# Down product of a SwiGLU layer: sums added into the residual by accumulating transfers, from copies made by ScalarE

## The chip, the cores and the metric

The kernel runs on one core of one Trainium2 chip. A core has a matrix engine (TensorE, PE in the profile; its weight loads are PEld), a vector engine (VectorE, DVE), a scalar engine (ScalarE, ACT), a general engine (GpSimd, POOL) and a synchronisation engine (SyncE, SP). Here SP only issues transfers (DMAs); the transfers themselves run on 16 DMA engines. Matrix products are written to PSUM, a small memory of 8 banks of 128 x 512 float32; everything else lies in SBUF. The metric is device time in microseconds (us) of one execution, lower is better.

## What is computed

A decoder layer: an input projection, two kinds of attention, an output projection and a feed-forward block, on 256 tokens of width 2048. The change lies in the feed-forward block (D_FF = 5632):

```
h = x + jnp.concatenate([gla_out, nsa_out], axis=-1) @ w_out
m = rms_norm(h, ffn_norm_g)
return h + (jax.nn.silu(m @ w_gate) * (m @ w_up)) @ w_down
```

All inputs and the output are float32.

## The kernel before

**Precision.** A float32 product is made from three matmuls of a faster 32-bit format: each operand is split into an upper part (copied into the format) and a lower part (what the copy lost), and upper x upper, upper x lower and lower x upper are summed in PSUM. `in_parts` (L563 to L565) does the split: ScalarE copies the upper part (L564), VectorE subtracts to get the lower part (L565).

**Tiling.** The residual `h_sb` is four tiles of [128, 2, 512] (two token tiles, 512 columns each). The hidden width 5632 is cut into 11 blocks of 512, numbered f = 0 to 10. The main loop (L1076 to L1082) runs gate_up(f) and then down(f-1); after gate_up(10) come down(9) and down(10).

**gate_up** (L949) walks over 8 pairs of 128-row weight tiles, in the order 0, 1, 2, 4, 3, 5, 6, 7 from f = 1 on (`ORDER`). Pairs 0, 2, 4, 5 and 6 are done with seven products in place of eight (a 2 x 2 scheme of Strassen's kind, 21 matmuls): for them VectorE also makes sums of weights (L983, L984, L985), and the split covers the weights (three quarters of the tile, here called w) and the sums (here called s, two splits). The other pairs take 24 matmuls and one split of the whole tile. At the end of the last seven-product pair the seven sums are combined from the PSUM banks (L1007 to L1012); at the end of the block the rest follows (L1019 to L1025). Those tiles come from the pool tag `f2` with 10 buffers of 512 columns.

**down** (L1041) multiplies one block of 512 hidden units by four column blocks n = 0 to 3 of `w_down`, 24 matmuls each, into two PSUM banks each (one per token tile). When a column block is done, VectorE adds each bank to the residual in place (L1055). In the last call the additions are made in halves of 256 columns, and each half is sent to the output (L1057).

**Weights** come in through `load4` (L928) into the tag `fraw`, 3 buffers of 1 MB, in two transfers of 512 KB (gate and up) or one of 1 MB (down); `two_parts` gives the 4 buffers of the tag `ftwo` for the split parts. A `fraw` buffer is free for the next load when VectorE and ScalarE have read it, an `ftwo` buffer when the matmuls that read it are done.

**Order.** When the kernel is built, the framework's scheduler puts the instructions of each engine in one fixed order, and the engine works them off in that order. An instruction that waits for another engine or for a transfer holds back what stands behind it. SP's transfers are issued in the order of the loads.

Of the kernel before, what the change touches and what calls it, by code (L numbers as in the profile page):

```python
# [11 lines left out]
AF = mybir.ActivationFunctionType  # L12
ALU = mybir.AluOpType
AX = mybir.AxisListType

P = 128
S = 256
NT = S // P
# [18 lines left out]
def kernel(  # L37
# [4 lines left out]
    nc = tc.nc  # L42
    act, mm = nc.scalar.activation, nc.tensor.matmul
    TT, TS, STT = nc.vector.tensor_tensor, nc.vector.tensor_scalar, nc.vector.scalar_tensor_tensor
# [12 lines left out]
    def slot(pool, tag, bufs, align=None):  # L57
        def f(shape, dt=F32):
            n_tiles[0] += 1
            return pool.tile([P] + list(shape), dt, tag=tag, bufs=bufs, name=f"{tag}_{n_tiles[0]}", align_bytes=align)  # L60
        return f
# [3 lines left out]
    g4, g2, g1, small = slot(gp, "g4", 24, LINE), slot(s2p, "g2", 13), slot(s1p, "g1", 7), slot(s1p, "sm", 12)  # L65

    def bank():
        n_tiles[0] += 1
        return pp.tile([P, 512], F32, tag="bank", name=f"bank_{n_tiles[0]}")
# [36 lines left out]
    last = {}  # L106
# [85 lines left out]
    def transpose(o, i, n=P):  # L192
        return nc.tensor.transpose(o, i, ident[:n, :n])  # L193
# [369 lines left out]
    def in_parts(hi, lo, ps):  # L563
        act(hi, ps, AF.Copy)  # L564
        TT(lo, ps, f32(hi), ALU.subtract)  # L565
# [273 lines left out]
    h_sb = []  # L839
# [32 lines left out]

    def pair_forms(pair, v):

        f = g2([4, P])
        a0, a1, b0, b1 = v[:, 0, :P], v[:, 0, P:], v[:, 1, :P], v[:, 1, P:]
        TT(f[:, 0], b1, a1, ALU.subtract)
        TT(f[:, 1], f[:, 0], b0, ALU.subtract)
        TT(f[:, 2], b0, b1, ALU.subtract)
        TT(f[:, 3], a0, f[:, 1], ALU.add)  # L880
        r = forms[pair] = g4([2, 4, P], F32R)
        in_parts(r[:, 0], r[:, 1], f)
# [32 lines left out]
    rf = kp.tile([P, NT], F32, name="rf")  # L915
    fw = {}

    def ffn_pools():
        nonlocal g2, small
        for pool in (wp, s2p, s1p, cp):  # L920
            pool.release()
        fr = ctx.enter_context(tc.tile_pool(name="fr", bufs=1, reuse_waits="tile"))
        fs = ctx.enter_context(tc.tile_pool(name="fs", bufs=1, reuse_waits="tile"))
        fp = ctx.enter_context(tc.tile_pool(name="fp", bufs=1, reuse_waits="tile"))
        fw["raw"], fw["two"] = slot(fr, "fraw", 3, LINE), slot(fp, "ftwo", 4, LINE)
        g2, small = slot(fs, "f2", 10), slot(fs, "fm", 4)

    def load4(parts):  # L928

        r, at = fw["raw"]([4, 512]) if fw else weight("raw", 4, 512, 3, F32), 0  # L930
        for mat, k0, nk, c0 in parts:
            nc.sync.dma_start(r[:, at:at + nk], mat[k0 * P:(k0 + nk) * P, c0:c0 + 512].rearrange("(k p) w -> p k w", p=P))
            at += nk
        return r

    def two_parts():
        w = fw["two"]([2, 4, 512], F32R)
        return w[:, 0], w[:, 1]
# [10 lines left out]
    def gate_up(fb, aTs, before):  # L949

        hi, lo = g4([4, S], F32R), g4([4, S], F32R)
        aTs.append((hi, lo))
        banks = {}

        def product(q, a, w, k):

            if q not in banks:
                banks[q] = bank()
                new = True
            else:  # L960
                new = False
            for i, (x, m) in enumerate(((a[0], w[k][0]), (a[0], w[k][1]), (a[1], w[k][0]))):
                todo[q] -= 1
                mm(banks[q], x, m, start=new and i == 0, stop=todo[q] == 0)  # L964

        def tokens(k, t):
            assert k in turned
            return tuple(x[k // 4][:, k % 4, t * P:(t + 1) * P] for x in (hT_h, hT_l))

        order, sevens = (ORDER0, FIRST7) if fb == 0 else (ORDER, PAIRS7)  # L970
        last7 = max(sevens, key=order.index)
        todo = dict.fromkeys((1, 5, 6, 7), 3 * len(sevens))
        todo.update(dict.fromkeys((2, 3, 4), 3 * len(sevens) + 6 * (8 - len(sevens))))
        todo[8] = 6 * (8 - len(sevens))
        for at, pair in enumerate(order):
            if fb == 0 and at == len(OLD):
                ffn_pools()
            a, b = 2 * pair, 2 * pair + 1
            r = load4([(m[0], a, 2, fb * FB) for m in (w_gate, w_up)])
            if pair in sevens:  # L980
                w = parts_of(r[:, 0:3])
                s1, s2 = g4([2, 512]), g4([2, 512])
                TT(s1, r[:, 1:3], r[:, 3:4].to_broadcast([P, 2, 512]), ALU.add)  # L983
                TT(s2[:, 0], s1[:, 1], r[:, 1], ALU.add)  # L984
                TT(s2[:, 1], s2[:, 0], r[:, 0], ALU.add)  # L985
                f = [tuple(forms[pair][:, i, j] for i in range(2)) for j in range(4)]
                product(1, tokens(b, 0), w, 1)
                yield 2
                product(2, tokens(a, 0), w, 0)
                yield 2  # L990
                product(3, f[3], w, 2)
                yield 2
                hi_, lo_ = two_parts()
                in_parts(hi_[:, 0:2], lo_[:, 0:2], s1)
                in_parts(hi_[:, 2:4], lo_[:, 2:4], s2)
                w = [(hi_[:, k], lo_[:, k]) for k in range(4)]
                for q, x, k in ((5, f[0], 0), (7, f[2], 1), (6, f[1], 2), (4, tokens(a, 1), 3)):
                    product(q, x, w, k)
                    yield 2
            else:  # L1000
                w = parts_of(r)
                for q, t, m in ((2, 0, 0), (3, 0, 1), (4, 1, 0), (8, 1, 1)):
                    for j in range(2):
                        product(q, tokens(a + j, t), w, 2 * m + j)
                        yield 2
            if pair == last7:
                q1, u, q5u, q7u, q57u = (g2([512]) for _ in range(5))  # L1007
                act(q1, banks[1], AF.Copy)
                TT(u, banks[6], q1, ALU.add)
                TT(q5u, banks[5], u, ALU.subtract)  # L1010
                TT(q7u, banks[7], u, ALU.add)
                TT(q57u, banks[5], q7u, ALU.subtract)  # L1012
                if before is not None:
                    urgent.append(before)
        if fb == 0:
            drain(urgent)
            rms(rf, ssh)
            TT(rf, rf, hback, ALU.mult)
        gs = []  # L1019
        for t, (g, gq, u_, uq) in enumerate(((q1, 2, q5u, 3), (q7u, 4, q57u, 8))):  # L1020
            TT(g, banks[gq], g, ALU.add)
            act(g, g, AF.Silu, scale=rf[:, t:t + 1])
            TT(u_, banks[uq], u_, ALU.add)
            STT(g, u_, rf[:, t:t + 1], g, ALU.mult, ALU.mult)
            gs.append(g)  # L1025
        turns[fb] = turn_act(gs, hi, lo)

    turns = {}

    def turn_act(gs, hi, lo):  # L1030
        for t in range(NT):
            ts = slice(t * P, (t + 1) * P)
            p = bank()
            for j in range(4):
                transpose(p[:, j * P:(j + 1) * P], gs[t][:, j * P:(j + 1) * P])
                if j % 2:
                    yield
            pv = p.rearrange("p (j s) -> p j s", j=4)
            in_parts(hi[:, :, ts], lo[:, :, ts], pv)

    def down(f0, aTs, last):  # L1041

        for m in range(2):
            banks = [[bank() for _ in range(NT)] for _ in range(2)]
            for f, (ah, al) in enumerate(aTs):
                end = f == len(aTs) - 1
                for i, n in enumerate((2 * m, 2 * m + 1)):
                    ws = parts_of(load4([(w_down[0], 4 * (f0 + f), 4, n * 512)]))
                    yield from chunk([banks[i]], ah, al, ws, f == 0, end, t_first=last and end)
                    if not end:  # L1050
                        continue
                    for t in range(NT):
                        for c in range(0, 512, 256 if last else 512):
                            cs = slice(c, c + (256 if last else 512))
                            TT(h_sb[n][:, t, cs], banks[i][t][:, cs], h_sb[n][:, t, cs], ALU.add)  # L1055
                            if last:
                                nc.sync.dma_start(out[t * P:(t + 1) * P, n * 512 + c:n * 512 + c + 256], h_sb[n][:, t, cs])  # L1057


    drive([proj(C_LR, ev_go(0), ((0, 256), (256, 272)), first_chunk)], 2)  # L1060
# [50 lines left out]
```

## Time and profile before

| | |
|---|---|
| median of 3 runs | 1134.25 us (1134.21 to 1136.03) |
| the profiled execution, its own time | 1134.1 us |
| its span, first to last instruction | 1132.4 us |
| granted clock of TensorE, mean | 0.999 of full |
| TensorE busy | 1120.4 us (99%) |
| VectorE busy | 965.9 us (85%) |
| ScalarE busy | 619.8 us (55%) |
| GpSimd busy | 23.6 us (2%) |
| bytes moved by transfers | 213.45 MB, 189 GB/s over the span |

From 516.78 us on, the profile repeats: one round is down(f-1) followed by gate_up(f+1), and nine such rounds follow each other until 1082.72 us, with down(9) and down(10) behind them. In the timelines below a row has start, duration, engine, line, operation, output and input with their shapes, and the number of instructions merged into the row; in brackets stands the idle time before it and what ended it.

### The profile page before, as it was taken

Reading aid. Unit: us, or ns where it says so; the run is one execution under the profiler, and the core shown is the slowest. Engines: PE = TensorE matmul, PEld = TensorE weight load, DVE = VectorE, ACT = ScalarE, POOL = GpSimd, SP = SyncE. Lnnn points to the kernel's source line nnn. Section 1 sums busy time; section 2 is a strip of 40 time slices with the busy share of each in tenths; the row PEclk is TensorE's granted clock in tenths of the full one; section 3 lists DMA queues with packets and bytes.
Section 4 is the critical chain, followed back from the end, with each engine's and each line's share of the span. In section 5 each row is a group of like instructions: output and inputs, shape, how many; then the busy total and the mean of one; then the engine's idle time right before and its main releaser. Section 6 shows DMA issues by size and latency. Waiting matters only on the chain.

```text
span 1132.4 us, 14359 instructions
## 1 busy us (share of the span) xinstructions
PE 1120.4 (99%) x5515; PEld 927.1 (82%) x5515; DVE 965.9 (85%) x1205; ACT 619.8 (55%) x763; POOL 23.6 (2%) x53
## 2 busy tenths in 40 slices
PE   9999999999999999999999999999999999999998
PEld 8888889998777777788888888888888888888886
DVE  6547779987588678999999999999999999999993
ACT  7654466544466486664555546364555555464640
POOL 3000000100000000000000000000000000000000
PEclk9999999999999999999999999999999999999999
DMA  7655543445853354556665656555565556565652
GB/s 269 233 186 186 186 149 114 152 151 152 299 182 112 112 186 149 184 193 219 221 224 180 225 180 233 186 202 193 199 208 200 207 166 223 185 243 168 196 211 75
DMA packets 110446, 213.45 MB, mean 189 GB/s; under 512 B 5109, under 2 KB 8217, under 8 KB 110378
## 3 DMA queue, kind: packets, MB, share of 16 engines
q1 hardware_dynamic: 110378, 212.54, 56.1%
q8 instruction: 43, 0.70, 0.2%
q14 instruction: 25, 0.20, 0.1%
HBM read 210.42 MB, written 2.10 MB: 188 GB/s over the span
## 4 chain that ended last, share of the span: by engine, by line
PE 89%; issue 4%; DVE 4%; DMA 1%; POOL 0%; SPq 0%; ACT 0%; POOLq 0%; DVEq 0%
PE bank L261 45%; PE bank L964 37%; PE bank L193 3%; PE bank L817 1%; PE bank L759 1%; DVE ftwo L565 1%; DMA raw<-in_w_out_dram 1%; DVE lo L130 1%; DMA g<-in_x_dram 1%; PE bank L513 1%; DVE g L515 0%; DVE g L518 0%; DVE g L490 0%; PE bank L675 0%; DVE g L489 0%
## 5 line engine op out<-in xcount | busy, mean ns | idle before, releaser
L964 PE MATMUL bank<-ftwo,g 128*128 128x512 f32 x1905 | 444.9, 392 | 1.3 <-DVE ftwo L565 1.1
L964 PEld LDWEIGHTS bank<-ftwo,g 128*128 128x128 f32 x1905 | 354.0, 188 | 75.4 <-DVE ftwo L565 2.2
L261 PE MATMUL bank<-hi,g 128*128 128x512 f32 (+3 forms) x1152 | 326.3, 366 | 0.8 <-DVE g L615 0.6
L564 ACT ACTIVATE ftwo<-fraw 128x1536 fp32r<-128x1536 f32 (+1 forms) x130 | 226.3, 1741 | 141.5 <-PE bank L261 41.2
L565 DVE TENSOR_TENSOR ftwo<-fraw,ftwo 128x1536 fp32r<-128x1536 f32 (+1 forms) x130 | 267.2, 2067 | 13.8 <-ACT ftwo L564 13.8
L261 PE MATMUL bank<-ftwo,g 128*128 128x512 f32 x1056 | 241.9, 389 | 0.0
L261 PEld LDWEIGHTS bank<-ftwo,g 128*128 128x128 f32 x1056 | 198.0, 188 | 41.6 <-DVE g L565 0.4
L261 PEld LDWEIGHTS bank<-hi,g 128*128 128x128 f32 x1152 | 199.3, 189 | 30.9 <-issue 2.3
L130 DVE TENSOR_TENSOR lo<-raw,hi 128x1024 fp32r<-128x1024 f32 (+3 forms) x125 | 151.4, 1218 | 74.5 <-ACT hi L129 74.0
L564 ACT ACTIVATE ftwo<-g 128x1024 fp32r<-128x1024 f32 x106 | 110.5, 1058 | 158.9 <-DVE g L983 75.2
L261 PE MATMUL bank<-lo,g 128*128 128x512 f32 (+1 forms) x576 | 195.3, 365 | 0.5 <-DVE lo L130 0.5
L129 ACT ACTIVATE hi<-raw 128x1024 fp32r<-128x1024 f32 (+3 forms) x125 | 131.3, 1056 | 109.3 <-PE bank L261 77.5
L565 DVE TENSOR_TENSOR ftwo<-g,ftwo 128x1024 fp32r<-128x1024 f32 x106 | 127.2, 1217 | 8.2 <-ACT ftwo L564 8.2
L261 PEld LDWEIGHTS bank<-lo,g 128*128 128x128 f32 x576 | 102.6, 189 | 15.0 <-issue 0.9
L1055 DVE TENSOR_TENSOR g<-bank,g 128x512 f32<-128x512 f32 (+1 forms) x96 | 59.3, 642 | 15.6 <-PE bank L261 14.7
L983 DVE TENSOR_TENSOR g<-fraw 128x1024 f32<-128x1024 f32 x53 | 64.5, 1216 | 0.0
L564 ACT ACTIVATE g<-bank 128x512 fp32r<-128x512 f32 (+1 forms) x50 | 29.2, 587 | 21.8 <-PE bank L193 12.5
L193 PE MATMUL bank<-ident,g 128*128 128x128 f32 (+2 forms) x214 | 38.4, 278 | 2.4 <-DVE g L548 1.1
L565 DVE TENSOR_TENSOR g<-bank,g 128x512 fp32r<-128x512 f32 (+1 forms) x50 | 33.6, 681 | 7.7 <-ACT g L564 7.4
L193 PEld LDWEIGHTS bank<-ident,g 128*128 128x128 f32 (+2 forms) x214 | 27.5, 142 | 12.3 <-issue 2.3
L985 DVE TENSOR_TENSOR g<-g,fraw 128x512 f32<-128x512 f32 x53 | 36.3, 685 | 0.6
L984 DVE TENSOR_TENSOR g<-g,fraw 128x512 f32<-128x512 f32 x53 | 36.3, 685 | 0.5
(192 smaller groups left out, 639.3 us busy)
## 6 DMA issues: line engine op xcount, KB each, us to landing
fraw<-in_w_down_dram SPq DMA_DIRECT2D x44, 1024.0 KB, 5.1
fraw<-in_w_gate_dram SPq DMA_DIRECT2D x86, 512.0 KB, 3.8
fraw<-in_w_up_dram SPq DMA_DIRECT2D x86, 512.0 KB, 4.7
raw<-in_w_in_dram SPq DMA_DIRECT2D x36, 1024.0 KB, 5.1
raw<-in_w_out_dram SPq DMA_DIRECT2D x16, 1024.0 KB, 5.1
raw<-in_w_in_dram SPq DMA_DIRECT2D x4, 1072.0 KB
g<-in_x_dram SPq DMA_DIRECT2D x7, 512.0 KB, 9.8
raw<-in_w_in_dram SPq DMA_DIRECT2D x3, 1056.0 KB, 11.4
```

What stands on the lines that cost most here:

```text
L129: act(h[:, i:i + n], r[:, k + i:k + i + n], AF.Copy)
L130: TT(o[:, i:i + n], r[:, k + i:k + i + n], f32(h[:, i:i + n]), ALU.subtract)
L193: return nc.tensor.transpose(o, i, ident[:n, :n])
L261: last["mm"] = mm(bk[t], a[:, k, t * P:(t + 1) * P], m[:, off:off + w], start=(first_ and k == 0 and i == 0), stop=(end and k == 3 and i = ...
L513: mm(p[:, j * P:(j + 1) * P], u, w, start=True, stop=True)
L564: act(hi, ps, AF.Copy)
L565: TT(lo, ps, f32(hi), ALU.subtract)
L964: mm(banks[q], x, m, start=new and i == 0, stop=todo[q] == 0)
L983: TT(s1, r[:, 1:3], r[:, 3:4].to_broadcast([P, 2, 512]), ALU.add)
L984: TT(s2[:, 0], s1[:, 1], r[:, 1], ALU.add)
L985: TT(s2[:, 1], s2[:, 0], r[:, 0], ALU.add)
L1055: TT(h_sb[n][:, t, cs], banks[i][t][:, cs], h_sb[n][:, t, cs], ALU.add)
```

## The change

The 80 additions of L1055 in all calls of `down` but the last are replaced. ScalarE copies the two banks of a column block into an SBUF tile `step` [128, 2, 512] (two buffers), and GpSimd issues a transfer of 512 KB from `step` to `h_sb[n]` that adds to what is there. To make room in the pool, the ten 2 KB buffers `f2` become two of 4 KB for `gate`, one of 4 KB for `up` and two of 4 KB for `step`; gate_up's combining steps are the same operations, written into halves of `gate` and `up`. The last call of `down` keeps its additions and its output transfers.

```
-        f = g2([4, P])
+        f = fw["up"]([4, P]) if fw else g2([4, P])
...
-        g2, small = slot(fs, "f2", 10), slot(fs, "fm", 4)
+        fw["up"], fw["step"] = slot(fs, "up", 1), slot(fs, "step", 2)
+        g2, small = slot(fs, "gate", 2), slot(fs, "fm", 4)
...
-                q1, u, q5u, q7u, q57u = (g2([512]) for _ in range(5))
-                act(q1, banks[1], AF.Copy)
-                TT(u, banks[6], q1, ALU.add)
-                TT(q5u, banks[5], u, ALU.subtract)
-                TT(q7u, banks[7], u, ALU.add)
-                TT(q57u, banks[5], q7u, ALU.subtract)
+                gate, up = g2([NT, 512]), fw["up"]([NT, 512])
+                act(gate[:, 0], banks[1], AF.Copy)
+                TT(up[:, 1], banks[6], gate[:, 0], ALU.add)
+                TT(up[:, 0], banks[5], up[:, 1], ALU.subtract)
+                TT(gate[:, 1], banks[7], up[:, 1], ALU.add)
+                TT(up[:, 1], banks[5], gate[:, 1], ALU.subtract)
...
+                    if not last:
+                        step = fw["step"]([NT, 512])
+                        for t in range(NT):
+                            act(step[:, t], banks[i][t], AF.Copy)
+                        nc.gpsimd.dma_start(h_sb[n], step, accum_op=ALU.add)
+                        continue
                     for t in range(NT):
-                        for c in range(0, 512, 256 if last else 512):
-                            cs = slice(c, c + (256 if last else 512))
+                        for c in range(0, 512, 256):
+                            cs = slice(c, c + 256)
                             TT(h_sb[n][:, t, cs], banks[i][t][:, cs], h_sb[n][:, t, cs], ALU.add)
-                            if last:
-                                nc.sync.dma_start(out[t * P:(t + 1) * P, n * 512 + c:n * 512 + c + 256], h_sb[n][:, t, cs])
+                            nc.sync.dma_start(out[t * P:(t + 1) * P, n * 512 + c:n * 512 + c + 256], h_sb[n][:, t, cs])
```

As built, the changed program has 80 instructions more on ScalarE, 80 fewer on VectorE and 40 transfers on GpSimd's queue, behind all its other work. TensorE's matmuls and SP's loads stand in the same order. On VectorE and ScalarE the fixed order around the pairs of gate_up moved as well. VectorE's order in a round, from pair 1 to pair 3 (lower parts written as "lo", the weight sums by line, old line numbers):

```
before: lo p0 s, lo p1, L1055 x2, L984 p2, lo p2 w, L985 p2, lo p2 s, L983 p4, lo p2 s, lo p4 w,
        L984 p4, L983 p5, L985 p4, L984 p5, lo p4 s x2, L985 p5, lo p3
after:  lo p0 s x2, L983 to L985 p2, L983 p4, L984 p4, lo p1, L985 p4, lo p2 w, lo p2 s x2, lo p4 w,
        L983 to L985 p5, lo p4 s x2, L983 p6, lo p3
```

ScalarE's copies for column blocks 0 to 3 stand ahead of its splits of pair 0 w, pair 0 s, pair 1 and pair 2 w.

More of the change, by code (lines that the diff above doesn't have):

```diff
@@ L1018, in gate_up, with turn_act @@
             TT(rf, rf, hback, ALU.mult)
-        gs = []
-        for t, (g, gq, u_, uq) in enumerate(((q1, 2, q5u, 3), (q7u, 4, q57u, 8))):
+        for t, (gq, uq) in enumerate(((2, 3), (4, 8))):
+            g, u = gate[:, t], up[:, t]
             TT(g, banks[gq], g, ALU.add)
             act(g, g, AF.Silu, scale=rf[:, t:t + 1])
[L1023 to L1026, printed above, removed]
+            TT(u, banks[uq], u, ALU.add)
+            STT(g, u, rf[:, t:t + 1], g, ALU.mult, ALU.mult)
+        turns[fb] = turn_act(gate, hi, lo)
     turns = {}
-    def turn_act(gs, hi, lo):
+    def turn_act(gate, hi, lo):
         for t in range(NT):
@@ L1034, in turn_act @@
             for j in range(4):
-                transpose(p[:, j * P:(j + 1) * P], gs[t][:, j * P:(j + 1) * P])
+                transpose(p[:, j * P:(j + 1) * P], gate[:, t, j * P:(j + 1) * P])
                 if j % 2:
```

## The prediction

> **What bounds the kernel now.** First the page's busy times, then the windows, cut at the rounds, then the chain of waits inside one round.
>
> ```profile
> PE 1120.4 (99%) x5515; PEld 927.1 (82%) x5515; DVE 965.9 (85%) x1205; ACT 619.8 (55%) x763; POOL 23.6 (2%) x53
> ```
>
> ```profile
> core 0: us, PE busy (x) PEld busy (x) DVE busy (x) ACT busy (x) POOL busy (x), PEclk, DMA share, GB/s
> 705.33:768.19 62.86, 62.86 (x282) 51.93 (x282) 59.98 (x58) 33.73 (x27) 0.00 (x0) 1.00 0.60 201
> ...
> 831.04:894.17 63.13, 63.13 (x282) 51.85 (x282) 60.57 (x59) 33.94 (x28) 0.00 (x0) 1.00 0.59 199
> ...
> 1082.72:1132.40 49.68, 44.60 (x201) 36.40 (x199) 28.54 (x37) 11.29 (x8) 0.00 (x0) 0.97 0.31 110
> ```
>
> ```profile
> 705.33 21.76 PE bank L261 x96
> 727.09 36.04 PE bank L964 x159
> 764.26 1.39 PE bank L964 x6
> 766.80 1.39 PE bank L964 x6
> 768.19 21.76 PE bank L261 x96
> ...
> 1087.38 39.95 PE bank L261 x176
> ```
>
> In a round TensorE never pauses: 96 matmuls in 21.76 us and 159 in 36.04 are 226.7 ns each, and the next round's first matmul starts as the last one ends. VectorE, from which the change takes work, is at 59.98 of 62.86 us, close to a bound without being one. Where it is less loaded (the last window, 28.54 of 49.68) the matmuls are no quicker: 176 in 39.95 us, 227.0 ns each. So less work on VectorE has nothing to shorten. What can be won is the little that is lost: 63.13 - 62.86 = 0.27 us in one round.
>
> The Trainium skill (Trainium Kernel Development and Optimization, Performance Expectations) warns that busy time of matmuls is a bad metric of distance to the roofline, since they are pipelined. By that rule 99% busy could hide waiting that VectorE causes. The trace does not agree: 226.7 ns in both halves of a round, and no less behind the rounds.
>
> **What is removed and added.** By form:
>
> ```profile
> L1055 DVE TENSOR_TENSOR g<-bank,g 128x512 f32<-128x512 f32 x80 | 53.3, 686 | 3.3 <-PE bank L261 2.4
> L1008 ACT ACTIVATE f<-bank 128x512 f32<-128x512 f32 x11 | 6.4, 584 | 1.2 <-PE bank L964 1.2
> ```
>
> Removed: 80 additions of 686 ns, 53.3 us of VectorE, 5.3 us a round. Worth nothing by itself, as said. Added: 80 copies from PSUM to SBUF of the kind of L1008, 80 x 0.584 = 46.7 us of ScalarE, 4.7 a round, which brings it to 38.4 of 62.86. Its time is no bound; its place may be. Write T for the start of a round's first matmul (705.33). A column block takes 24 x 0.2267 = 5.44 us, so the copies can run at T + 5.44, 10.88, 16.32 and 21.76, and ScalarE stands still for them. Behind them wait its splits:
>
> ```profile
> 710.86 1.49 ACT L564 ACTIVATE ftwo<-fraw 128x1536 fp32r<-128x1536 f32 x1 [2.91 <-issue]
> 718.19 1.06 ACT L564 ACTIVATE ftwo<-g 128x1024 fp32r<-128x1024 f32 x1 [5.84 <-DVE g L983]
> ...
> 721.74 1.92 ACT L564 ACTIVATE ftwo<-fraw 128x2048 fp32r<-128x2048 f32 x1 [1.11 <-PE bank L261]
> 727.46 1.49 ACT L564 ACTIVATE ftwo<-fraw 128x1536 fp32r<-128x1536 f32 x1 [3.80 <-PE bank L261]
> ```
>
> These are pair 0's w and first s, pair 1 and pair 2's w; all but the s already began right when the same column blocks ended (T + 5.5, 16.4, 22.1), because they need the buffer that those matmuls free. Each now comes some 1 us later: pair 2 at T + 21.85 + 2 x 0.55 = 23.0. TensorE wants pair 2 at T + 21.76 + 45 x 0.2267 = 31.96. Free. The PSUM banks that the copies release are wanted no sooner: the last pair of them, free at T + 23.0, by the seventh product of gate_up at T + 21.76 + 18 x 0.2267 = 25.84.
>
> Also added: 40 transfers of 512 KB from SBUF to SBUF that add. The trace has no transfer from GpSimd and none that adds. Two numbers matter: how long one takes to land (L), and how much time of the 16 DMA engines it eats (a). A round loads 12 MB (8 pairs and 4 column blocks) at a share of 0.60 of 62.86 us: 37.7 us, 3.1 us a MB. As a plain copy, a = 1.6 us is the low end; since the destination must be read too, twice the reading gives a = 3.1, and this I take, as nearer to what such a transfer does. For L:
>
> ```profile
> fraw<-in_w_gate_dram SPq DMA_DIRECT2D x86, 512.0 KB, 3.8
> fraw<-in_w_up_dram SPq DMA_DIRECT2D x86, 512.0 KB, 4.7
> ...
> g<-in_x_dram SPq DMA_DIRECT2D x7, 512.0 KB, 9.8
> ```
>
> 3.8 us is the low end, 9.8 (512 KB in a crowd of loads) the high end; I take about 3.8 + 1.6 = 5.4, for the second reading.
>
> The Trainium skill (Collectives: The Full Stack, The bandwidth ceiling: the fold count and why AG ≠ RS ≠ AR) says that an adding step runs at half the rate of a copy, because two sources are read. That speaks against this change; by it a is 3.1 too. No run before shows it.
>
> `step` has two buffers: the copy of block 2 at T + 16.4 needs block 0's transfer, issued at about T + 6.7, landed. Free up to L = 9.6; and up to about 12.9 TensorE would not feel it (block 3's first copy, 0.58, behind block 1's transfer of T + 12.3, for the bank wanted at T + 25.84). At 5.4, nothing. On GpSimd's queue nothing stands behind a transfer but the next one, 5.44 us later.
>
> **Where the stall goes.** What I hold to decide is VectorE's order around pairs 4, 5 and 3. Before:
>
> ```profile
> 724.05 2.28 DVE L565 TENSOR_TENSOR ftwo<-fraw,ftwo 128x2048 fp32r<-128x2048 f32 x1
> 726.45 1.37 DVE L1055 TENSOR_TENSOR g<-bank,g 128x512 f32<-128x512 f32 x2
> ...
> 728.98 1.76 DVE L565 TENSOR_TENSOR ftwo<-fraw,ftwo 128x1536 fp32r<-128x1536 f32 x1 [0.56 <-ACT ftwo L564]
> 730.65 0.69 DVE L985 TENSOR_TENSOR g<-g,fraw 128x512 f32<-128x512 f32 x1
> ...
> 736.93 1.22 DVE L983 TENSOR_TENSOR g<-fraw 128x1024 f32<-128x1024 f32 x1
> ...
> 739.27 2.35 DVE L565 TENSOR_TENSOR ftwo<-g,ftwo 128x1024 fp32r<-128x1024 f32 x2
> 741.54 0.68 DVE L985 TENSOR_TENSOR g<-g,fraw 128x512 f32<-128x512 f32 x1
> 742.15 3.95 DVE L565 TENSOR_TENSOR ftwo<-fraw,ftwo 128x2048 fp32r<-128x2048 f32 x2
> ```
>
> ```profile
> 726.36 0.37 SPq L932 DMA_DIRECT2D fraw<-in_w_gate_dram  x1
> ...
> 731.41 0.37 SPq L932 DMA_DIRECT2D fraw<-in_w_gate_dram  x1
> 731.82 0.47 SPq L932 DMA_DIRECT2D fraw<-in_w_up_dram  x1
> ```
>
> The row at 724.05 is pair 1's lower part, 728.98 pair 2's, 736.93 pair 5's first sum, 742.15 pair 3's lower part (2.28 of the 3.95), done at T + 39.1. Pair 3's second matmul needs it at T + 21.76 + 88 x 0.2267 = 41.7: a margin of 2.6 us, the smallest that I find in gate_up. SP loads pair 3 when pair 1's lower part is done (726.36) and pair 5 when pair 2 is through (731.41, T + 26.1), so pair 5's up half lands at about 731.82 + 4.7 = T + 31.2, just before its use at T + 31.6.
>
> After, with the durations of these rows: pair 2's split on ScalarE is 0.9 later, done at T + 24.5; its lower part, with L985 now done ahead, ends at T + 24.5 + 1.76 = 26.3, and pair 5's load goes out as before. VectorE is through with pair 2's s and pair 4's w at T + 26.3 + 2.35 + 1.76 = 30.4 and now stands at pair 5's three sums, with pair 4's s, pair 6's first sum and pair 3 behind them. If pair 5 lands at T + 31.3 + d, pair 3's lower part is there 1.22 + 2 x 0.69 + 2.35 + 1.22 + 2.28 = 8.45 later, at T + 39.7 + d. So TensorE stalls by d - 2.0 in each round.
>
> And d is there. Block 3's transfer goes out at about T + 23.2. Pair 3's load is later than before, next to it, since pair 1's lower part now stands behind L983 and L984 of pair 4: VectorE gets to these at about T + 12.1 (block 1's copies) + 1.06 + 2.35 (pair 0's s) + 2.6 (pair 2's sums) = 18.1, and they need pair 4's load, which goes out when pair 0 is through (T + 6.7 + 1.49 + 1.76 + 2.6 = 12.5) and lands 0.41 + 4.7 = 5.1 later at best, beside block 1's transfer. So pair 1 is done, and pair 3 loads, at T + 18.1 + 1.22 + 0.69 + 2.28 = 22.3, or 23.5 with crowding, where it was T + 21.0. Pair 3 takes 3.1 us of engine time and pair 5 follows 2.7 to 3.9 us behind, so block 3's a is passed on to pair 5 less some 0.5: d = 1.1 for a = 1.6, 2.6 for a = 3.1. The stall is 0 at the low end and 0.6 us at the value taken.
>
> **Sum.** Nine rounds have a gate_up behind a changed down: 9 x 0.6 = 5.4 us. Gains taken as 0 (0.27 at most in sight). The profiled execution's own 1134.1 (its span and 1.7 around it) + 5.4 = 1139.5; it lies 0.15 below the median shown, less than the runs differ.
>
> **Rivals.**
> 1. *All of it hides* (not slower). If a is under 2.5 us, or the margin was read too small, nothing reaches TensorE and the rounds stay 62.86 us: 1134.2. For it: TensorE has no gap anywhere in a round, and a lies between 1.6 and 3.1. Against it: the margins were already that small, and four new transfers a round fall into the half in which VectorE now waits for loads.
> 2. *The adding transfers are several times dearer.* With L = 9.8 and the fixed part of a plain landing (3.8 - 1.6 = 2.2) off, a would be 7.6: four of them and the loads make 30.4 + 37.7 = 68.1 us of engine time in 62.86, and rounds become at least 5.2 longer: 9 x 5.2 = 47, 1181. It decides from a = (62.86 - 37.7) / 4 = 6.3 on. For it: nothing in the trace bounds an adding transfer. A wait for `step` beyond L = 12.9 would have the same look on ScalarE, 1 us a round for each us.
> 3. *VectorE's relief counts.* All pauses that the windows show in the rounds are 0.27 us, so 1133.8 at best; over 0.2% would need matmuls closer than 226.7 ns.
>
> **Chances.** Forecast (a stall of some tenths to 1.3 us a round, up to 1146) 0.42; rival 1 0.38; dearer, from there up to rival 2, 0.15; rival 3 or another gain 0.05. About 0.2%, 2.3 us, is what a measurement of this kernel can tell from no change. Faster by more 0.05, within 0.38, slower 0.57. The forecast's own range is 1136.5 to 1146; the range goes down to rival 1 and up to a of about 5 (d 4.5, 2.5 us a round, 9 x 2.5 = 22): 1133.5 to 1156.
>
> **What would show it.** Right: rounds longer than 62.86 by a few tenths, with TensorE idle at pair 3 (or pair 4's s), released by VectorE's L565, and VectorE idle before pair 5's sums, released by a load of gate or up; loads of gate and up landing later than 3.8 and 4.7. Rival 1: rounds of 62.85. Rival 2: a DMA share near 1, or ScalarE idle before its copies, released by a transfer. VectorE should fall to about 54.7 a round, ScalarE rise to 38.4. Wrong at the root: a stall in the first 516 us, or matmul spacing that changes.

## The result, and the profile after

| | before | after |
|---|---|---|
| median, runs side by side | 1135.03 us (4 runs) | 1144.22 us (4 runs, 1142.31 to 1145.50) |
| the profiled execution, its own time | 1134.1 us | 1143.9 us |
| its span | 1132.4 us | 1142.1 us |
| nine rounds | 565.94 us | 576.77 us |
| behind the rounds | 49.68 us | 48.63 us |

After over before is 1.0079, 95% interval 1.0061 to 1.0097: the changed kernel is 9.2 us slower. The span grew by 9.7 us; the nine rounds by 576.77 - 565.94 = 10.83, and the end behind them is 1.05 shorter. What lies ahead of the rounds is as it was (they begin at 516.70 us, before at 516.78).

First from the page of the changed kernel: busy times, the queue of the adding transfers, the groups that are new or that changed, and the issues (the last number is the median time from issue to landing).

```profile
PE 1122.8 (98%) x5515; PEld 925.3 (81%) x5515; DVE 920.2 (81%) x1125; ACT 661.2 (58%) x843; POOL 58.0 (5%) x93
...
q0 software_dynamic: 5760, 20.97, 9.7%
...
L984 DVE TENSOR_TENSOR g<-fraw 128x1024 f32<-128x1024 f32 x53 | 64.7, 1221 | 54.7 <-DMA fraw<-in_w_up_dram 54.7
L1056 ACT ACTIVATE step<-bank 128x512 f32<-128x512 f32 x80 | 47.5, 598 | 95.6 <-PE bank L261 81.2
L1057 POOL DMA_DIRECT2D g<-step x40 | 34.5, 863 | 644.4 <-ACT step L1056 641.3
...
fraw<-in_w_gate_dram SPq DMA_DIRECT2D x86, 512.0 KB, 4.2
fraw<-in_w_up_dram SPq DMA_DIRECT2D x86, 512.0 KB, 5.2
g<-step POOLq DMA_DIRECT2D x40, 512.0 KB, 6.3
```

VectorE is down by 45.7 us and TensorE did not gain from it. An adding transfer takes 0.097 x 1142.1 / 40 = 2.77 us of the 16 DMA engines' time and lands after 6.3 us. Loads of gate and up land 0.4 to 0.5 us later than before (3.8 and 4.7), at the median. VectorE's first weight sum of a pair (L984 now, L983 before) has waited 54.7 us for loads of up; before, no such wait stands among its waits from 500 us on.

The windows of the changed kernel, cut at the rounds (columns as before):

```profile
core 0: us, PE busy (x) PEld busy (x) DVE busy (x) ACT busy (x) POOL busy (x), PEclk, DMA share, GB/s
516.70:582.23 65.53, 63.44 (x283) 51.78 (x282) 58.58 (x52) 38.82 (x37) 3.63 (x4) 1.00 0.78 243
582.23:646.30 64.07, 63.15 (x282) 51.86 (x282) 55.37 (x50) 37.90 (x35) 3.43 (x4) 1.00 0.74 229
646.30:710.41 64.11, 63.15 (x282) 51.86 (x282) 55.44 (x50) 37.97 (x35) 3.44 (x4) 1.00 0.75 231
710.41:774.22 63.81, 63.15 (x282) 51.85 (x282) 55.45 (x50) 37.94 (x35) 3.43 (x4) 1.00 0.74 231
774.22:838.15 63.93, 63.18 (x282) 51.85 (x282) 55.34 (x50) 37.94 (x35) 3.43 (x4) 1.00 0.73 229
838.15:903.00 64.85, 64.39 (x287) 52.38 (x285) 55.24 (x50) 38.85 (x36) 3.44 (x4) 1.00 0.74 226
903.00:966.31 63.31, 62.52 (x278) 51.19 (x278) 55.28 (x50) 37.05 (x35) 3.43 (x4) 1.00 0.74 233
966.31:1029.61 63.30, 63.18 (x282) 51.85 (x282) 55.84 (x50) 37.98 (x35) 3.43 (x4) 1.00 0.75 234
1029.61:1093.47 63.86, 63.14 (x282) 51.86 (x282) 55.35 (x50) 37.95 (x35) 3.43 (x4) 1.00 0.74 231
1093.47:1142.10 48.63, 44.56 (x200) 36.39 (x199) 23.40 (x29) 15.50 (x16) 3.43 (x4) 0.99 0.55 155
```

The cut at 903.00 lies five matmuls inside the seventh round, which begins at about 901.6; by its own first matmul the sixth round lasts 63.5 us and the seventh 64.7.

The round at T = 710.41 lasts 63.81 us in place of 62.86. DMA share is up from 0.60 to 0.74. The chain of waits, which before was TensorE alone, runs through that round like this (start, duration, what; short pieces are left out):

```profile
710.41 5.46 PE bank L261 x24
716.38 1.49 ACT ftwo L564
717.90 1.76 DVE ftwo L565
719.65 1.15 DVE g L984
722.73 8.21 DMA fraw<-in_w_up_dram
731.04 1.24 DVE g L984
733.06 2.05 issue
735.79 1.68 DVE ftwo L565
737.90 6.44 DMA fraw<-in_w_up_dram
744.44 1.24 DVE g L984
749.30 1.22 DVE g L984
750.52 2.21 DVE ftwo L565
752.78 16.39 PE bank L965 x71
```

Read it as a sentence: pair 0's split (716.38, 717.90) and its sums end, which frees the buffer for pair 4's load (722.73); that takes 8.21 us; VectorE's sums of pair 4 wait for it; pair 1's and pair 2's lower parts stand behind them, and when pair 2's is read (735.79) pair 5's load goes out (737.90) and takes 6.44; VectorE's sums of pair 5 wait for that, with pair 3's lower part (750.52) behind them; and for that TensorE waits. VectorE's and TensorE's own timelines of the same round show the three waits in brackets:

```profile
731.04 1.23 DVE L984 TENSOR_TENSOR g<-fraw 128x1024 f32<-128x1024 f32 x1 [3.10 <-DMA fraw<-in_w_up_dram]
732.91 2.28 DVE L565 TENSOR_TENSOR ftwo<-fraw,ftwo 128x2048 fp32r<-128x2048 f32 x1
...
744.44 1.23 DVE L984 TENSOR_TENSOR g<-fraw 128x1024 f32<-128x1024 f32 x1 [3.04 <-DMA fraw<-in_w_up_dram]
...
750.44 3.95 DVE L565 TENSOR_TENSOR ftwo<-fraw,ftwo 128x2048 fp32r<-128x2048 f32 x2
```

```profile
752.78 16.39 PE L965 MATMUL bank<-ftwo,g 128*128 128x512 f32 x71 [0.66 <-DVE ftwo L565]
```

TensorE's matmuls stand still for 0.66 us at pair 3. The 71 matmuls behind take 16.39 us where 71 x 0.2267 is 16.10, 0.29 more: 62.86 + 0.66 + 0.29 = 63.81. The two parts are seen as one at the weight loads (PEld). These overlap with the matmuls (51.85 and 63.15 us busy in this round of 63.81), so the load that needs VectorE's lower part is due a little before its matmul. In this round it waited 1.1 us. Over all rounds (us in total, times, longest):

```profile
PEld bank L965 <- DVE ftwo L565: 11.3, 10, 1.9
...
PE bank L965 <- DVE ftwo L565: 7.0, 9, 1.5
```

The nine rounds grew by 10.83 us, which is about what the weight loads waited and more than the matmuls did.

### The profile page after: what moved, and what is told of

It reads as the page before. It is cut to its first block, busy times and chain, and to the rows that moved or that the text cites. A ratio compares the mean times of both kernels' runs of the same rounds, so it can differ in the third digit from the quotient of the medians.

```text
span 1142.1 us, 14462 instructions
## 1 busy us (share of the span) xinstructions
PE 1122.8 (98%) x5515; PEld 925.3 (81%) x5515; DVE 920.2 (81%) x1125; ACT 661.2 (58%) x843; POOL 58.0 (5%) x93
## 4 chain that ended last, share of the span: by engine, by line
PE 60%; DVE 16%; DMA 13%; issue 7%; ACT 2%; SPq 1%; POOL 0%; DVEq 0%; ACTq 0%; POOLq 0%
PE bank L261 34%; PE bank L965 20%; DMA fraw<-in_w_up_dram 11%; DVE ftwo L565 7%; DVE g L984 4%; PE bank L193 3%; DVE g L986 2%; DVE g L985 1%; PE bank L817 1%; ACT ftwo L564 1%; PE bank L759 1%; DMA fraw<-in_w_down_dram 1%; PE bank L513 1%; DMA raw<-in_w_out_dram 1%; DMA g<-in_x_dram 1%
## 5 line engine op out<-in xcount | busy, mean ns | idle before, releaser
L261 PEld LDWEIGHTS bank<-ftwo,g 128*128 128x128 f32 x1056 | 197.9, 188 | 42.3 <-DVE g L565 1.2
L261 PEld LDWEIGHTS bank<-hi,g 128*128 128x128 f32 x1152 | 199.3, 189 | 30.7 <-issue 2.3
L564 ACT ACTIVATE ftwo<-g 128x1024 fp32r<-128x1024 f32 x106 | 108.1, 1054 | 108.4 <-PE bank L965 86.7
L984 DVE TENSOR_TENSOR g<-fraw 128x1024 f32<-128x1024 f32 x53 | 64.7, 1221 | 54.7 <-DMA fraw<-in_w_up_dram 54.7
L1056 ACT ACTIVATE step<-bank 128x512 f32<-128x512 f32 x80 | 47.5, 598 | 95.6 <-PE bank L261 81.2
L1057 POOL DMA_DIRECT2D g<-step x40 | 34.5, 863 | 644.4 <-ACT step L1056 641.3
L565 DVE TENSOR_TENSOR g<-bank,g 128x512 fp32r<-128x512 f32 (+1 forms) x50 | 33.6, 681 | 7.0 <-ACT g L564 6.9
L985 DVE TENSOR_TENSOR g<-g,fraw 128x512 f32<-128x512 f32 x53 | 36.6, 690 | 1.4
```

The lines of the kernel that those rows point to most:

```text
L261: last["mm"] = mm(bk[t], a[:, k, t * P:(t + 1) * P], m[:, off:off + w], start=(first_ and k == 0 and i == 0), stop=(end and k == 3 and i = ...
L1056: act(step[:, t], banks[i][t], AF.Copy)
L1057: nc.gpsimd.dma_start(h_sb[n], step, accum_op=ALU.add)
```

## The experiments

Eleven kernels, each timed against the kernel before. All times are medians, the ratio is to the kernel before on the same chip, whose median was 1134.90 us beside e1 to e4, 1134.83 beside e5 to e8 and 1134.68 beside e9 to e11. The ratio isn't taken from the two medians and differs from theirs by up to 0.1%. The fixed order of VectorE is that of the changed kernel in e1, e3, e8, e9, e10 and e11, nearly that of the kernel before in e5, and that of the kernel before in e4.

### Is it the order, the copies, the buffers or the transfers?

**e3_no_transfer.** The transfers are left out, all else stays.

```
-                        nc.gpsimd.dma_start(h_sb[n], step, accum_op=ALU.add)
```

> The changed kernel without its 40 adding transfers: ScalarE makes the copies and nothing adds them, so the down products are left out of the residual (but for the last one); buffers and VectorE's order as changed. Theory A: pair 5's load lands about 2.7 us earlier in a round, as before, and the new order costs nothing or little: 1133.5 to 1137. Rival O: 1142 to 1145. Rival S: 1142 to 1145. Rival C: 1134 to 1135, with no stall at all.

1133.55 us, ratio 0.9994 (0.9983 to 1.0005). Order, copies, smaller buffers: together they cost nothing. A round, from the windows of this kernel:

```profile
706.95:769.80 62.85, 62.85 (x282) 51.92 (x282) 55.46 (x50) 37.99 (x35) 0.00 (x0) 1.00 0.60 201
```

62.85 us with TensorE busy throughout and VectorE at 55.46. So VectorE's relief, which this kernel has as well, is worth nothing either (rival 3).

**e4_buffers_only.** The additions are back on VectorE, and only the new buffers of gate and up stay.

```
-                        step = fw["step"]([NT, 512])
...
-                            act(step[:, t], banks[i][t], AF.Copy)
-                        nc.gpsimd.dma_start(h_sb[n], step, accum_op=ALU.add)
+                            TT(h_sb[n][:, t], banks[i][t], h_sb[n][:, t], ALU.add)
```

> Only the part of the change in the buffers of gate and up (one gate pair and one up pair in place of ten single tiles): the additions stand on VectorE again, with no copies and no transfers; VectorE's order is that of the kernel before. Theory A, O and C: as before, 1134 to 1135.5. If the smaller buffers cost (part of rival S): 1137 to 1144.

1134.42 us, ratio 0.9992 (0.9984 to 1.0001): the buffers cost nothing.

**e1_plain_copy.** The transfers copy and do not add.

```
-                        nc.gpsimd.dma_start(h_sb[n], step, accum_op=ALU.add)
+                        nc.gpsimd.dma_start(h_sb[n], step)
```

> The changed kernel, but its 40 transfers copy instead of adding, so the residual is overwritten and the sum over the down products is left out; everything else, VectorE's order too, is as in the changed kernel. Theory A (the adding transfers delay the loads of gate and up, and VectorE's new order makes pair 3's lower part wait for pair 5's load): a transfer falls from 2.8 to about 1.6 us of engine time, so pair 5's load lands about 1 us earlier in a round and most of the stall of 1.1 us a round goes: 1135 to 1139. Rival O (the order alone, with or without transfers): unchanged, 1142 to 1145. Rival S (the copies on ScalarE, the smaller gate, up and step buffers, or the wait for step): unchanged, 1142 to 1145. Rival C (any crowding, whatever the order): between, by the share of engine time, about 1139.

1134.56 us, ratio 0.9991 (0.9982 to 1.0001): the whole loss is gone, more than was expected. From the page of this kernel, the queue and the landing:

```profile
q0 software_dynamic: 5760, 20.97, 4.8%
...
L1057 POOL DMA_DIRECT2D g<-step x40 | 21.7, 543 | 646.1 <-ACT step L1056 642.6
...
g<-step POOLq DMA_DIRECT2D x40, 512.0 KB, 4.3
```

A plain transfer takes 0.048 x 1131.4 (its span) / 40 = 1.36 us of engine time, an adding one 2.77, 2.04 times as much. The bytes are the same. At the median the loads of gate and up land no sooner here than in the changed kernel (4.6 and 5.5 us against 4.2 and 5.2), so the median doesn't tell which loads do harm. VectorE's waits for loads at L984 do: 31.5 us here, 54.7 in the changed kernel.

**e8_two_copies.** Each plain copy is made twice, so that the engine time is that of the adding transfers again.

```
                         nc.gpsimd.dma_start(h_sb[n], step)
+                        nc.gpsimd.dma_start(h_sb[(n + 2) % 4], step)
```

> The kernel with plain copies in place of the adding transfers, each copy made twice (the second into the residual tile two blocks on), so the sum over the down products is left out; VectorE's order as changed. The engine time a block is then that of one adding transfer, about 2.7 us against 2.8. If engine time is what delays the loads: 1140 to 1145, loads of pair 4 and 5 as late as in the changed kernel. If it is the adding itself (a transfer that reads its destination back holds the engines or queues beyond its engine time): 1134 to 1138.

1148.72 us, ratio 1.0131 (1.0116 to 1.0146), more than either theory had. From the page of this kernel:

```profile
q0 software_dynamic: 11520, 41.95, 9.2%
```

0.092 x 1145.1 / 40 = 2.63 us of engine time a block, and the loss is back without any adding; it is larger than in the changed kernel (13.9 against 9.2 us). So the loss needs no adding: transfers that take up the engines for as long bring it back. (Packets and bytes are twice those of the changed kernel; engine time is what the two share.) That the loss is larger still isn't explained by engine time alone. Of the 3.0 us between the two profiled spans (1145.1 and 1142.1), 1.7 lie in the nine rounds and 1.2 ahead of them, where the two programs don't differ. In this kernel ScalarE also waits for `step`, in its waits from 500 us on:

```profile
ACT step L1056 <- DMA g<-step: 17.5, 6, 3.9
```

17.5 us in six waits; in the changed kernel it was one wait of 3.0. That wait makes ScalarE's splits later, but what share of the loss it has was not tried.

### Which order, which transfers?

**e5_old_order_adds.** The changed kernel with 80 additions on VectorE into a tile that nothing reads, which gives VectorE nearly the old order (and its old load, 964.3 us).

```
+        fw["junk"] = slot(fs, "junk", 1)([512], BF16)
...
                             act(step[:, t], banks[i][t], AF.Copy)
+                            TT(fw["junk"].rearrange("p (a b) -> p a b", a=2), banks[i][t].rearrange("p (a b) -> p a b", a=2), f32(ah[:, 0:2]), ALU.add)
```

> The changed kernel with 80 additions of 128x512 put back on VectorE at their old places, into a spare tile that nothing reads, only to give VectorE nearly the order and the load of the kernel before; copies, adding transfers and buffers stay as changed. Theory A (crowding and the new order together): pair 4's sums no longer stand ahead of pair 1's lower part, so most of the loss goes although the transfers stay: 1134.5 to 1139. Rival C (the adding transfers cost in any order): 1142 to 1146. Rival V (VectorE, at 60 of 63 us again and now beside later loads, has no slack): 1144 to 1160.

1137.07 us, ratio 1.0023 (1.0013 to 1.0033): most of the loss goes although all the transfers are there and VectorE has more to do. In the profiled execution one round alone, the second, is much longer (64.83 us). So neither the transfers alone (this kernel: 2.2 us, with VectorE's old load) nor the order alone (e3: nothing) makes the 9.2; it takes both.

**e6_pair4_behind, e2_sums_behind, e7_both_behind.** The changed kernel with VectorE's three sums held, by a constraint on the order, behind a lower part: pair 4's behind pair 1's (e6), pair 5's behind pair 3's (e2), or both (e7).

```
+                with behind(last.get("lo") if fb > 1 and pair == 4 else None):
                     TT(s1, r[:, 1:3], r[:, 3:4].to_broadcast([P, 2, 512]), ALU.add)
                     TT(s2[:, 0], s1[:, 1], r[:, 1], ALU.add)
                     TT(s2[:, 1], s2[:, 0], r[:, 0], ALU.add)
```

(`last["lo"]` is the subtraction of the last full pair; in e2 the condition is pair 5, in e7 pairs 4 and 5.)

> The changed kernel with one constraint: VectorE's three sums of pair 4 stand behind pair 1's lower part; pair 5's stay where the change has them, ahead of pair 3's lower part. If the hold at pair 4 is the first cause (it makes pair 1, pair 3's load and all that follows late): pair 3's load goes out near T + 21 to 22 again, the stall at pair 3 goes, 1134.5 to 1138. If pair 5's place alone decides, as the prediction's formula has it: still 1140 to 1144. Between, about 1139, if each hold gives half.

> The changed kernel with one constraint more: VectorE's three sums of pair 5 stand behind pair 3's lower part; transfers, copies and buffers as changed. Theory A: TensorE no longer waits at pair 3; the sums of pair 4 still wait for their load ahead of pair 1's lower part, so a little stays: 1135 to 1139, VectorE's lower part of pair 3 done before T + 41.7 in the rounds. Rival O says the same, 1135 to 1139. Rival C (the engines are crowded, and some operand comes late in any order): 1142 to 1145, with the stall moved to pair 5 or 6. Rival S: 1142 to 1145.

> The changed kernel with both constraints: pair 4's sums behind pair 1's lower part and pair 5's behind pair 3's. Theory A: no stall of TensorE at pair 3, 1134 to 1137; the loss that stayed with pair 5's sums alone moved (1137.9, a load of w_down late at the end of two rounds) goes if it came from pair 4's hold, and stays at 1137 to 1139 if it comes from pair 5's sums freeing their load buffer later. Rival C: 1142 to 1145.

e6: 1135.73 us, ratio 1.0008 (1.0000 to 1.0017). e2: 1137.88 us, 1.0017 (1.0005 to 1.0030). e7: 1135.98 us, 1.0012 (1.0003 to 1.0021). Moving pair 4's sums by one place is enough: within the 0.2% it is the kernel before. The round at T = 707.81 of e6, from its windows and VectorE's timeline:

```profile
707.81:770.67 62.86, 62.86 (x282) 51.95 (x282) 55.69 (x50) 37.94 (x35) 3.44 (x4) 1.00 0.76 234
```

```profile
726.61 2.29 DVE L565 TENSOR_TENSOR ftwo<-fraw,ftwo 128x2048 fp32r<-128x2048 f32 x1 [1.32 <-ACT ftwo L564]
729.01 1.23 DVE L985 TENSOR_TENSOR g<-fraw 128x1024 f32<-128x1024 f32 x1
...
739.72 1.22 DVE L985 TENSOR_TENSOR g<-fraw 128x1024 f32<-128x1024 f32 x1 [2.02 <-DMA fraw<-in_w_up_dram]
...
745.72 3.95 DVE L565 TENSOR_TENSOR ftwo<-fraw,ftwo 128x2048 fp32r<-128x2048 f32 x2
```

Pair 1's lower part comes first, pair 4's sums then find their load there, and pair 3's lower part begins at T + 37.9 where it was T + 40.0. The DMA share is 0.76: the crowd is as dense as ever, but in this round TensorE doesn't wait for it. In the first round of e6 it still does: there pair 4's load takes 10.18 us, and the round lasts 64.84. With pair 5's sums held back (e2) TensorE doesn't wait at pair 3 either, but time is lost at another place, at the end of the first round and of the fifth. The chain of e2, at the end of the fifth:

```profile
822.07 2.31 DVE ftwo L565
824.39 5.93 DMA fraw<-in_w_down_dram
830.43 1.92 ACT ftwo L564
```

There a load of `w_down` is late, and ScalarE does its split ahead of what the end of gate_up needs: from 770.32 two rounds take 126.50 us in place of 2 x 62.86 = 125.72. The chain of e7 has the same piece (6.37 us from 824.75; two rounds in 126.93), and that of e6 has none in its rounds. So with pair 4's sums out of the way it comes with pair 5's place. The times don't settle it: e7's median is the lower one (1135.98 against 1137.88), while of the two profiled executions e7's is the longer (1136.65 against 1135.90). It would fit that the sums, done later, free their load buffer later; this was not measured by itself.

**e9_blocks_0_3, e10_blocks_1_2, e11_blocks_0_1_2.** The changed kernel with the transfers of the named column blocks alone.

```
-                        nc.gpsimd.dma_start(h_sb[n], step, accum_op=ALU.add)
+                        if n in (0, 3):
+                            nc.gpsimd.dma_start(h_sb[n], step, accum_op=ALU.add)
```

> The changed kernel with the adding transfers of column blocks 0 and 3 alone; those of blocks 1 and 2, which run beside pair 4's load, are left out, and with them their part of the residual. VectorE's order as changed. If pair 4's load is what counts (8.2 us in the changed kernel, 5.1 without crowding: 3.1 us off the path to pair 3): 1134 to 1136. If block 3's transfer, beside pair 5's load, is what counts, as the prediction has it: d stays 2.3 and the stall stays near 0.6 to 1.1 us a round, 1139 to 1143.

> The mirror: the adding transfers of blocks 1 and 2 alone, those of 0 and 3 left out. If block 3's transfer is what counts (the prediction's d): 1134 to 1136. If pair 4's load is: the 3.1 us stay, pair 5's 1.7 us go; since the stall is about 1.1 us a round, 1135 to 1139 with little or no stall left, and pair 4's load still at 7 to 8 us.

> Only block 3's adding transfer is left out. By the prediction's formula (d is block 3's engine time less 0.5): d goes to 0, no stall, 1134 to 1136. If pair 4's load is the main cause: pair 5's load gains 1 to 1.7 us and the rest stays, 1136 to 1141.

e9: 1136.40 us, ratio 1.0011 (1.0000 to 1.0022). e10: 1135.67 us, 1.0007 (0.9999 to 1.0016). e11: 1140.50 us, 1.0046 (1.0033 to 1.0060). Without block 3's transfer 5.8 of the 9.2 us stay; without blocks 1 and 2 it is 1.7, without 0 and 3 it is 1.0. So the reading by block 3's transfer fails in e9 and e11. Pair 4's load alone isn't enough either: in e10 its sums begin nearly as late as in the changed kernel (T + 20.4 against 20.6), and the loss is 1.0. No one transfer carries the loss; it grows with how many there are, 1.0 and 1.7 us with two, 5.8 with three, 9.2 with four.

One round of each kernel in one table, in us from its T. The columns come from the rows of VectorE's and SP's timelines as shown above (pair 3's lower part ends 2.28 after its row begins), and the first row from the kernel before. Rounds of one kernel differ: those of e9 so much that it is left out, and e11's row is one of its mild ones, since its first round (65.30) and its eighth (65.10) hold most of its loss:

| kernel | T | pair 4's sums begin | pair 5's up half issued | pair 5's sums begin | pair 3's lower part done | round |
|---|---|---|---|---|---|---|
| before | 705.33 | 27.1 | 26.5 | 31.6 | 39.1 | 62.86 |
| e3, no transfer | 706.95 | 17.4 | 26.0 | 30.7 | 38.9 | 62.85 |
| e1, plain copies | 705.32 | 18.9 | 26.0 | 31.6 | 40.2 | 62.86 |
| e6, pair 4 behind | 707.81 | 21.2 | 26.0 | 31.9 | 40.2 | 62.86 |
| e10, blocks 1 and 2 | 708.04 | 20.4 | 27.3 | 32.6 | 40.9 | 62.86 |
| e11, blocks 0 to 2 | 709.66 | 20.5 | 27.4 | 33.3 | 41.6 | 63.08 |
| after | 710.41 | 20.6 | 27.5 | 34.0 | 42.3 | 63.81 |
| e8, two copies | 713.43 | 21.7 | 28.6 | 34.6 | 42.9 | 64.39 |

TensorE's matmul wants pair 3's lower part at T + 41.7, but the round grows sooner: by what the part comes later than T + 41.4 (0.2 in e11, 0.95 in the changed kernel, 1.5 in e8). The 0.3 in between is the weight load, which is due ahead of its matmul: in this round of e11 no matmul waits, and a weight load waits 0.33.

No kernel of these is faster than the one before beyond what can be told.

## Why the prediction came out as it did

**Where it was right.** Forecast was a loss of 5.4 us, measured 9.2. The mechanism is the one that was forecast: loads later by the adding transfers, VectorE held at sums of pair 4 and of pair 5 by its new order, pair 3's lower part late, TensorE waiting there. e3, e5 and e6 show that it takes both the transfers and the order. For the matmul's wait the margin holds to a tenth: pair 5's sums were to hurt from T + 31.3 + 2.0 = 33.3 on; in the rounds of the table e11 stands at 33.3 and none of its matmuls waits, the changed kernel at 34.0 waits 0.66 (forecast 0.6), e8 at 34.6 waits 1.23.

**VectorE's relief is worth nothing, the copies hide, the buffers are free**: shown by e3 and e4. VectorE fell to 55.45 a round (forecast 54.7) and ScalarE rose to 37.94 (38.4). A copy took 598 ns (584 taken).

**Engine time and landing.** a was 2.77 (3.1 taken), L 6.3 at the median (5.4 taken). `step` was waited for once, 3.0 us, as good as never. The rule of the Trainium skill (Collectives: The Full Stack, The bandwidth ceiling: the fold count and why AG ≠ RS ≠ AR) that an adding step runs at half the rate since it reads two sources agrees with the 2.04 measured here. The page says further that the addition itself is not what costs; no run here separates the addition from the second read.

**The step that was mis-sized** is the last term of the sum, "Nine rounds have a gate_up behind a changed down: 9 x 0.6 = 5.4 us". The wait of the matmul was sized rightly in the round at 710.41, but the round loses more, 0.95: the margin was read at the matmul (T + 41.7), and the weight load wants the part at T + 41.4. That is 0.3 in each of nine rounds. The rest is that the part came later than forecast: it was to be done at T + 42.3 (39.7 + 2.6) and was done at T + 44.0 (the first round), 42.6, 42.6, 42.3, 42.4, 42.0, 43.2, 41.8 and 42.4, on the mean at 42.6. Over the 62.86 the rounds lost 2.67, 1.21, 1.25, 0.95, 1.07, 0.6, 1.8, 0.44 and 1.00, together 11.0. In each that is within a tenth what the part came later than T + 41.4. Two pieces from the chain of the changed kernel, one of the first round and one of the end of the sixth:

```profile
532.48 10.98 DMA fraw<-in_w_up_dram
...
887.02 7.82 DMA fraw<-in_w_down_dram
```

In the first round pair 4's load takes 10.98 us, and TensorE waits at pair 4's sums too (0.64 us there, 1.46 at pair 3). At the end of the sixth a load of `w_down` comes late, as in e2, and VectorE starts the seventh about 1 us behind. Against that stand 1.05 us won behind the rounds, which no part of the prediction had. TensorE needs 44.6 us there in both kernels; from VectorE's last addition, behind which only output transfers are left, to the end of the span it is 5.04 us before and 4.03 after. Why these end sooner was not tried.

**A part that was right by two errors.** d, pair 5's delay, was to be 2.6 and was 34.0 - 31.3 = 2.7. But the prediction took all of it from block 3's transfer (a less 0.5) and had "pair 5's load goes out as before". It went out 1.0 later (T + 27.5 against 26.5): pair 4's load took 8.21 us where 4.7, or 5.9 with crowding, was reckoned, so pair 1's lower part was done at T + 24.8 (22.3 to 23.5 reckoned) and pair 2's at T + 27.1 (26.3). And pair 5's load itself took 6.44 in place of 4.7. In e11, where block 3 is gone, d is still 2.0: only 0.7 of the 2.7 is block 3's (over the nine rounds pair 5's sums begin at 33.6 on the mean there and at 34.3 in the changed kernel, the same difference). That pair 4's hold is the first cause is shown by e6. With the a that was measured, 2.77, the prediction's own formula gives d = 2.3, a stall of 0.3 a round and a loss of 2.4 us. That the wait came out near 0.6 is in part luck.

**The rivals.** All hides (rival 1): false, but by little: e1 has a = 1.36, and seven of its nine rounds last 62.86 (the others 63.19 and 63.13; the kernel before has one of 63.13). It needed a below 2.5 by the prediction's own bound, and a was 2.77. Several times dearer (rival 2): false, a is far from 6.3. VectorE's relief (rival 3): false, by e3.

## What to carry to other kernels

Where one engine is back to back, as TensorE is here, work taken from another was worth nothing, and what counted is what the new form of that work collides with: here 40 transfers with the loads of the next stage. On an engine with a fixed order, look at what stands behind the first instruction that needs a late load: an order that is harmless while loads are on time makes a chain out of a small delay, and one constraint on it took the loss away (e6) with all the transfers in place. A margin can be read from a profile to some tenths, but for a matmul's weights it has to be read at the weight load: here that is 0.3 us less, and about 3 us over nine rounds. Rounds differ too, so the sum over rounds wants a wider upper side.

## What was not expected of the hardware

An adding transfer from SBUF to SBUF costs 2.04 times the engine time of a plain one (2.77 against 1.36 us for 512 KB) and GpSimd takes longer to issue it, 863 against 543 ns (L1057 in the pages of the changed kernel and of e1). Two plain copies in place of one adding transfer cost the kernel more (13.9 us) than the adding one (9.2), at slightly less engine time. And pair 3's lower part was due at its weight load 0.3 us before its matmul (T + 41.4 against 41.7), so a stall of the matmuls of 0.66 us went with a round longer by 0.95.
